# Reordering one pair's attention work beside the projections, and narrower passes for the values' products

## The chip, the cores and the metric

One core of a Trainium2 chip. The metric is the device time of one execution in microseconds (us). TensorE (PE) multiplies and transposes into PSUM; its weight loads are shown as PEld. VectorE (DVE), ScalarE (ACT) and GpSimd (POOL) do elementwise work, SyncE (SP) issues most of the DMAs.

## The reference

A trunk of two layers on one sequence of 512 positions with 1024 features, in float32. Layer 0 mixes by dilated window attention, layer 1 by a short gated convolution; each is followed by a squared-ReLU MLP, and each sub-layer has an RMS norm ahead of it and a residual behind it. The change is in the attention:

```python
qkv = (h @ w_qkv).reshape(B, S, 3, 3, 16, 64)      # group, q/k/v, head, feature
for g in range(3):                                  # dilations 1, 4, 16
    q = partial_rope(rms_norm(qkv[:, :, g, 0], q_gain[g]), cos, sin)
    k = partial_rope(rms_norm(qkv[:, :, g, 1], k_gain[g]), cos, sin)
    num, den, mx = dilated_group(q, k, qkv[:, :, g, 2], dilation[g], radius[g])
w = exp(mx - max over groups of mx)
o = (sum of w * num) / (sum of w * den)
y = o @ w_o
```

`dilated_group` is a softmax over a band of 129 keys (fewer for dilation 16) without its last division: the numerator, the sum of the exponentials and the row maximum.

## The kernel before

Every float32 operand is split into two parts of TensorE's float32r type, `h` (high) and `l` (low), and a product is the sum of three matmuls: high by high, high by low, low by high. ScalarE makes the high part, VectorE the low one (`split`), GpSimd the low one of the weights.

**The stream.** TensorE's main work is a list of units (`add_unit`). A unit is one projection of all 512 rows: eight k-tiles, four row tiles, three matmuls each. Units are cut into blocks of one or two k-tiles, for which weights are loaded (SP's queue) and split ahead. `clock` counts positions: one unit of position is 2048 moving columns by three matmuls, so 16 matmuls of 384 columns (a "projection" below is one of these), or 12 of 512. The 16 heads are taken in 8 pairs; a pair has three units of six positions: A (q of group 0, k of group 0, q of group 1), B (k of group 1, q and k of group 2) and V (the values). Behind pair 7 come the output projections (512 columns), then the MLP, the convolution and the second MLP.

**The tasks.** All other work is put into a heap of tasks with a position (`at`, `put`), and `run_tasks` issues them between the matmuls when their position is reached. Each engine executes in the order of issue, so the positions set the order in every engine's queue. The positions are in `PLACES`: one row for pair 0, one for pairs 1 to 6, one for pair 7. They are counted from the end of A (`tA`) for `sqA`, `rsA`, `mulA`, `TA`, and from the end of B (`tB`, `tS`, the start of V) for the rest. So a pair's attention runs beside its own V and the next pair's A and B.

A pair's tasks, in order: `sqB` squares and row sums; `rsB` (the reciprocal root by Newton steps, 12 small VectorE instructions); `mulB` for four row tiles: the norm product on VectorE (L372), then the rotary step, four small instructions (L377 to L380) on GpSimd for the first `pB` row tiles, on VectorE for the rest, in the buffers `tmpR1` and `tmpR2`, two each; `TB`: transposes and splits of k1, q2, k2 (`qk_fill`, PSUM tiles `st`, three buffers). `S0` twice: scores of group 0 for two of four query blocks, both heads, by matmuls with 64 contraction rows, and on VectorE the masked scores with their maxima (L446); `E0`: exponentials on ScalarE (L465). `X1`, `X2`: maxima and sums of group 0 go from its layout into that of the other groups: `spread` on VectorE (L423), then `swap` on TensorE (L432, 32-column stationary) and a copy; I call this the first exchange. `S12`, `E12`: the same for groups 1 and 2. `W1` to `W4`: the weights of the groups, carried back by a second exchange. `N12`, `N0`: the exponentials times these weights, on GpSimd and VectorE. `PT` (8 times, head `h`, part `i`): four transposes and a split into `pth` and `ptl`; `PV`: the values' products into the single PSUM tile `o`, parts 0 and 1 for group 0 (values `v0`, moved through DRAM), 2 and 3 for groups 1 and 2. The stationary operand of a `PV` matmul is 128 columns wide, high and low half of the values side by side, so that the low half's product comes out in partitions 64 to 127 of `o`; behind a head's last part ScalarE copies those to `tmpO` (L545) and VectorE adds them into `oT` (L546). `qA`, `qB`, `pA`, `pB`, `pN` choose engines, `vA`, `vB` who empties the projections' PSUM (`rawA`, `rawB`).

In pair 0, the setup runs beside it: among it eight fills of the zero halves of k1 and k2 (`zeros`, L269 and L270, VectorE) at positions 9.0 to 11.1. Ahead of the output projections, `split_o` splits `oT`; the last pair's at one position before the end of the first projection unit, directly ahead of the block that reads it.

Of the kernel before, what the change touches and what calls it, by code (L numbers as in the profile page):

```python
# [11 lines left out]
F32 = mybir.dt.float32  # L12
# [23 lines left out]
def _constants():  # L36
# [10 lines left out]
    for n, b in enumerate((0, 1, 3)):  # L47
# [10 lines left out]


PLACES = [  # L60
    dict(sqA=0.52, rsA=0.95, mulA=2.62, dmA=0.05, TA=4.92, dT=0.16, sqB=0.08, rsB=1.22, mulB=1.5, dmB=0.08, TB=4.51, S0=0.4,
         dS=1.15, E0=1.0, X=3.2, lX=0.35, S12=6.05, dS12=0.41, E12=6.8, dE12=0.22, W=8.7, lW=0.25, N12=9.05, N0=9.4, dN=0.04,
         P=10.0, dP=0.75, lP=1.2, qA=0, qB=0, pA=3, pB=3, pN=1, vA=0, vB=8, xq=3.57, dxq=0.29, xs=6.25, lg=2.48, dlg=0.43, tb=4.26, dtb=0.21, gc=8.63),
    dict(sqA=0.02, rsA=0.87, mulA=1.79, dmA=0.28, TA=4.62, dT=0.19, sqB=0.17, rsB=0.8, mulB=1.07, dmB=0.12, TB=3.57,
         S0=0.42, dS=0.92, E0=1.0, X=3.0, lX=0.35, S12=6.0, dS12=0.24, E12=6.6, dE12=0.2, W=8.4, lW=0.25, N12=8.75,
         N0=9.1, dN=0.04, P=9.7, dP=0.75, lP=1.2, qA=0, qB=0, pA=0, pB=3, pN=1, vA=0, vB=12),
    dict(sqA=0.02, rsA=0.8, mulA=1.1, dmA=0.5, TA=4.12, dT=0.02, sqB=0.19, rsB=0.89, mulB=1.15, dmB=0.33, TB=3.4, S0=1.44,
         dS=1.15, E0=2.0, X=4.3, lX=0.3, S12=5.0, dS12=0.25, E12=5.6, dE12=0.2, W=7.3, lW=0.25, N12=7.65, N0=8.0,
         dN=0.04, P=8.4, dP=0.45, lP=0.63, qA=0, qB=0, pA=3, pB=2, pN=1, vA=0, vB=9),
]  # L70


# [1 line left out]
def trunk_kernel(ctx, tc, x, norm1, norm2, wqkv, qgain, kgain, wo, win, conv, wout, w1, w2, c_rope, c_m0, c_m12, out):  # L74
    nc = tc.nc
    pe, act, dve, pool, sync = nc.tensor, nc.scalar, nc.vector, nc.gpsimd, nc.sync
    ctx.enter_context(tc.manual_schedule())

    def ptile(p, shape, dt, name, **kw):
        return p.tile(shape, dt, name=name, **kw)  # L80
# [82 lines left out]
    ab = open_pool("attn", bufs=1)  # L163
# [16 lines left out]
    xs = dram.tile([KT, 128, S], F32, name="xs")  # L180
# [189 lines left out]
    def norm_mul(raw, stt, ng, tab, r, eng):  # L370
        v = raw[r].rearrange("p a (h d) -> p (a h) d", d=64)
        dve.tensor_mul(v, v, stt[:, 2, ng * r:ng * r + ng, None].to_broadcast([128, ng, 64]))  # L372
        rot = v[:, :, 0:16]
        t1 = ptile(ab, [128, 8, 16], F32, "tmpR1", bufs=2)
        t2 = ptile(ab, [128, 8, 16], F32, "tmpR2", bufs=2)
        tb = tab.rearrange("p s r w h d -> p s r (w h) d")
        eng.tensor_mul(t1[:, :ng], rot, tb[:, 0, r])  # L377
        eng.tensor_mul(t2[:, :ng, 0:8], v[:, :, 8:16], tb[:, 1, r, :, 0:8])  # L378
        eng.tensor_mul(t2[:, :ng, 8:16], v[:, :, 0:8], tb[:, 1, r, :, 8:16])  # L379
        eng.tensor_add(rot, t1[:, :ng], t2[:, :ng])  # L380
# [36 lines left out]

    N0, D0, N0S, N12, D0S, D12, F0S, F12, NM, EX, F0 = 0, 1, 2, 3, 4, 5, 6, 7, 8, 9, 12

# [14 lines left out]

    def S0(bp):
        ps = [ptile(psT, [128, 512], F32, "st") for _ in range(2)]
# [6 lines left out]
        for h in range(2):  # L443
            for b2 in range(2):
                b = 2 * bp + b2
                dve.tensor_tensor_reduce(out=sm0[:, h, b], in0=ps[h][:, 256 * b2:256 * b2 + 256],  # L446
                                         in1=msk0[:, (0, 1, 1, 2)[b]], scale=1.0, scalar=3.0e38, op0=ALU.add, op1=ALU.min,
                                         accum_out=mx(N0)[:, 4 * h + b:4 * h + b + 1])

# [43 lines left out]
    def weights_back(p):  # L493
        ps = swap(st[p].pop("sp1"), 8)
        dve.tensor_copy(mx(F0).rearrange("p (h b) -> p h b", h=2), ps)
# [28 lines left out]
    def PV(p, h, i, first, last):  # L524

        hi, lo = st[p].pop(("pt", h, i))
        if first:
            st[p]["o"] = ptile(psO, [128, 512], F32, "o")
        o = st[p]["o"]
        ops = []  # L530
        if i < 2:
            for j in (2 * i, 2 * i + 1):
                ov = o.rearrange("p (r b c) -> p b r c", r=4, c=32)
                ov = ov[:, j:j + 2] if j < 3 else ov[:, 0:4:3]
                ops += [(ov, st[p]["v0"][:, j, h], t[:, 256 * (j % 2):256 * (j % 2) + 256]) for t in (hi, lo)]
        else:
            v = st[p]["v"].rearrange("p r g h s d -> p r g h (s d)")
            for r in range(4):
                c = slice(128 * r, 128 * r + 128)
                ops += [(o[:, c], v[:, r, i - 1, h], t[:, c]) for t in (hi, lo)]  # L540
        for q, (out_, stat, mov) in enumerate(ops):
            pe.matmul(out_, stat, mov, start=first and q == 0, stop=last and q == len(ops) - 1, skip_group_check=True)  # L542
        if last:
            t1 = ptile(ab, [64, 512], F32, "tmpO")
            act.copy(t1, o[64:128])  # L545
            dve.tensor_add(oT[p][64 * h:64 * h + 64], o[0:64], t1)  # L546
# [38 lines left out]
    def attn_tasks(p, tA, tB, c):  # L585


        tS = tB

        def put(pos, name, fn, *needs):  # L590
            def go():
                for n in needs:
                    need(*n)
                fn()
                mark(name, p)
            at(pos, go)

        for r in range(4):
            put(tA + c["sqA"] + 0.25 * r, "sqA", lambda r=r: norm_sq(rawA, stA, 6, r, r < c["qA"]), ("evA", p, 4))
        put(tA + c["sqA"] + c["rsA"], "rsA", lambda: norm_rs(stA, 6), ("sqA", p, 4), ("stats", 0, 1))  # L600
        for r in range(4):
            put(tA + c["mulA"] + c["dmA"] * r, "mulA", lambda r=r: norm_mul(rawA, stA, 6, tabA, r, pool if r < c["pA"] else dve), ("rsA", p, 1), ("tables", 0, 6))
        for i, nm in enumerate(("q0", "k0", "q1")):
            put(tA + c["TA"] + c["dT"] * i, "TA", lambda i=i, nm=nm: qk_fill(rawA, i, nm, i), ("mulA", p, 4), ("cols", 0, 1),
                ("S0", p - 1, 2), ("S12", p - 1, 4))
        for r in range(4):
            put(tB + c["sqB"] + 0.25 * r, "sqB", lambda r=r: norm_sq(rawB, stB, 6, r, r < c["qB"]), ("evB", p, 4))
        put(tB + c["sqB"] + c["rsB"], "rsB", lambda: norm_rs(stB, 6), ("sqB", p, 4))
        for r in range(4):
            put(tB + c["mulB"] + c["dmB"] * r, "mulB", lambda r=r: norm_mul(rawB, stB, 6, tabB, r, pool if r < c["pB"] else dve), ("rsB", p, 1))  # L610
        for i, nm in enumerate(("k1", "q2", "k2")):
            put(tB + c["TB"] + c["dT"] * i, "TB", lambda i=i, nm=nm: qk_fill(rawB, i, nm, 3 + i), ("mulB", p, 4),
                ("S12", p - 1, 4))
        for i in range(2):
            put(tS + c["S0"] + c["dS"] * i, "S0", lambda i=i: S0(i), ("TA", p, 3), ("PT", p - 1, 8), ("gains", 0, 11))
            for n in range(4):
                put(tS + c["E0"] + c["dS"] * i + 0.15 * n, "E0", lambda i=i, n=n: exps(0, n // 2, 2 * i + n % 2), ("S0", p, i + 1))

        def sp0():
            st[p]["sp0"] = spread(mx(N0, 2), 16)  # L620

        put(tS + c["X"], "X1", sp0, ("E0", p, 8), ("perm", 0, 1))
        put(tS + c["X"] + c["lX"], "X2", lambda: stats_over(p), ("X1", p, 1), ("N0", p - 1, 8))
        for r in range(4):
            put(tS + c["S12"] + c["dS12"] * r, "S12", lambda r=r: S12(r), ("TB", p, 3), ("PT", p - 1, 8))
            for h in range(2):
                put(tS + c["E12"] + c["dE12"] * (2 * r + h), "E12", lambda h=h, r=r: exps(1, h, r), ("S12", p, r + 1))
        w = tS + c["W"]
        put(w, "W1", weigh1, ("E12", p, 8), ("X2", p, 1))
        put(w + 0.1, "W2", weigh2, ("W1", p, 1))  # L630
        put(w + c["lW"], "W3", lambda: weigh3(p), ("W2", p, 1))
        put(w + c["lW"] + c["lX"], "W4", lambda: weights_back(p), ("W3", p, 1))
        for n in range(8):
            put(tS + c["N12"] + c["dN"] * n, "N12", lambda n=n: pnorm(1, n // 4, n % 4, n % 4 >= c["pN"]), ("W3", p, 1))
            put(tS + c["N0"] + c["dN"] * n, "N0", lambda n=n: pnorm(0, n // 4, n % 4, n % 4 >= c["pN"]), ("W4", p, 1))
        for n, (h, i) in enumerate(((0, 2), (0, 3), (0, 0), (0, 1), (1, 2), (1, 3), (1, 0), (1, 1))):
            s = tS + c["P"] + c["dP"] * n
            put(s, "PT", lambda h=h, i=i: PT(p, h, i), ("N12" if i > 1 else "N0", p, 8))
            put(s + c["lP"], "PV", lambda h=h, i=i, n=n: PV(p, h, i, n % 4 == 0, n % 4 == 3), ("PT", p, n + 1), ("evV", p, 4),
                ("v0", p, 1))  # L640
# [3 lines left out]
    c = PLACES[0]  # L644
# [317 lines left out]
    for i, b in enumerate(blocks):  # L962
# [4 lines left out]
        ops = b["emit"]([ready.pop(b["first"] + q) for q in range(b["n"])])  # L967
# [28 lines left out]
```

## Time and profile before

| | us |
|---|---|
| median of 3 timed runs | 1557.04 (1555.07 to 1557.34) |
| the profiled execution, its time | 1546.28 |
| its span, first to last instruction | 1544.2 |
| TensorE busy | 1486.8 |
| VectorE busy | 679.4 |
| ScalarE busy | 662.8 |
| GpSimd busy | 725.5 |

Times within the trace count from the span's start. Matmuls are pipelined: a row's duration is longer than the distance from its start to the next start, and the distance is what it costs. An idle time in brackets names what ended it. L numbers are lines of the kernel.

### The profile page before, as it was taken

Reading aid. Unit: us, or ns where it says so; the run is one execution under the profiler, and the core shown is the slowest. Engines: PE = TensorE matmul, PEld = TensorE weight load, DVE = VectorE, ACT = ScalarE, POOL = GpSimd, SP = SyncE. Lnnn points to the kernel's source line nnn. Section 1 sums busy time; section 2 is a strip of 40 time slices with the busy share of each in tenths; the row PEclk is TensorE's granted clock in tenths of the full one; section 3 lists DMA queues with packets and bytes.
Section 4 is the critical chain, followed back from the end, with each engine's and each line's share of the span. In section 5 each row is a group of like instructions: output and inputs, shape, how many; then the busy total and the mean of one; then the engine's idle time right before and its main releaser. Section 6 shows DMA issues by size and latency. Waiting matters only on the chain.

```text
span 1544.2 us, 22344 instructions
## 1 busy us (share of the span) xinstructions
PE 1486.8 (96%) x7772; PEld 1302.1 (84%) x7772; DVE 679.4 (44%) x1522; ACT 662.8 (43%) x1364; POOL 725.5 (47%) x760
## 2 busy tenths in 40 slices
PE   8799999999999988999999999999999999999998
PEld 8699999999999987788888888888887888888887
DVE  5747565656657475363112131474347420121222
ACT  5355564645555545444433242343334443433320
POOL 3544444445363554354445444445544444444542
PEclk9899999999999999999999999999999999999999
DMA  5432323222232322433332333233332233233332
GB/s 141 140 90 62 100 66 91 83 85 87 75 93 59 100 78 75 134 97 96 94 98 96 96 96 99 89 86 93 105 116 84 89 103 96 96 96 96 96 96 82
DMA packets 163292, 144.75 MB, mean 94 GB/s; under 512 B 13748, under 2 KB 123116, under 8 KB 163180
## 3 DMA queue, kind: packets, MB, share of 16 engines
q1 hardware_dynamic: 162892, 143.06, 30.7%
q8 instruction: 61, 1.00, 0.3%
q14 instruction: 51, 0.42, 0.1%
q10 hardware_dynamic: 288, 0.27, 0.1%
HBM read 134.89 MB, written 8.39 MB: 93 GB/s over the span
## 4 chain that ended last, share of the span: by engine, by line
PE 77%; issue 8%; DVE 7%; POOL 4%; DMA 1%; ACT 1%; SPq 1%; POOLq 0%; ACTq 0%; DVEq 0%
PE g L127 71%; POOL wl L292 2%; PE o L542 2%; PE st L456 1%; PE st L515 1%; PE st L389 1%; DMA wraw<-in_a_wqkv 1%; POOL tmpR L377 1%; DVE sqa L698 0%; DVE spread L423 0%; SPq L565 0%; POOL tmpR L379 0%; POOL tmpR L378 0%; DVE hgBl L700 0%; DMA sm<-in_x 0%
## 5 line engine op out<-in xcount | busy, mean ns | idle before, releaser
L292 POOL TENSOR_TENSOR wl<-wraw,wh 128x512 fp32r<-128x512 f32 (+1 forms) x542 | 636.8, 1196 | 737.0 <-ACT wh L291 729.3
L291 ACT CAST wh<-wraw 128x512 fp32r<-128x512 f32 (+1 forms) x542 | 297.6, 570 | 493.6 <-PE g L127 398.4
L127 PE MATMUL g<-hgBh,wl 128*128 128x512 f32 x704 | 274.6, 390 | 0.0
L127 PE MATMUL g<-hgBh,wh 128*128 128x512 f32 x704 | 274.6, 390 | 0.0
L127 PE MATMUL g<-hgBl,wh 128*128 128x512 f32 x704 | 274.4, 390 | 0.0
L127 PE MATMUL g<-wh,hgh 128*128 128x384 f32 x768 | 267.0, 348 | 0.1
L127 PE MATMUL g<-wl,hgh 128*128 128x384 f32 x768 | 265.8, 346 | 0.0
L127 PE MATMUL g<-wh,hgl 128*128 128x384 f32 x768 | 262.8, 342 | 1.9 <-DVE hgl L306 1.7
L788 DVE SCALAR_TENSOR_TENSOR zr<-g,R 128x512 f32<-128x512 f32 x64 | 44.1, 691 | 293.1 <-PE g L127 293.0
L127 PEld LDWEIGHTS g<-hgBh,wl 128*128 128x128 f32 x704 | 132.5, 188 | 27.8
L127 PEld LDWEIGHTS g<-hgBh,wh 128*128 128x128 f32 x704 | 132.5, 188 | 27.6
L127 PEld LDWEIGHTS g<-hgBl,wh 128*128 128x128 f32 x704 | 132.6, 188 | 27.5
L127 PEld LDWEIGHTS g<-wh,hgl 128*128 128x128 f32 x768 | 146.1, 190 | 3.2 <-DVE hgl L306 3.0
L127 PEld LDWEIGHTS g<-wl,hgh 128*128 128x128 f32 x768 | 146.2, 190 | 2.0
L127 PEld LDWEIGHTS g<-wh,hgh 128*128 128x128 f32 x768 | 145.8, 190 | 1.2 <-ACT hgh L304 0.4
L805 DVE TENSOR_TENSOR acc<-g,acc 128x512 f32<-128x512 f32 x32 | 22.1, 691 | 138.2 <-PE g L127 138.2
L292 DVE TENSOR_TENSOR ptl<-st,pth 128x512 fp32r<-128x512 f32 x64 | 44.1, 689 | 79.2 <-ACT pth L291 78.7
L291 ACT CAST pth<-st 128x512 fp32r<-128x512 f32 x64 | 37.6, 587 | 95.4 <-PE st L515 95.3
L465 ACT ACTIVATE sm<-sm,mxs 128x256 f32<-128x256 f32 x128 | 63.7, 499 | 27.5 <-DVE mxs L446 24.0
L127 PE MATMUL g<-z0h,wh 128*128 128x512 f32 x192 | 74.7, 389 | 0.0
L127 PE MATMUL g<-z0l,wh 128*128 128x512 f32 x192 | 74.7, 389 | 0.0
L127 PE MATMUL g<-z0h,wl 128*128 128x512 f32 x192 | 74.7, 389 | 0.0
(222 smaller groups left out, 2369.9 us busy)
## 6 DMA issues: line engine op xcount, KB each, us to landing
wraw<-in_mlp_w SPq DMA_DIRECT2D x256, 256.0 KB
wraw<-in_a_wqkv SPq DMA_DIRECT2D x128, 128.0 KB
wraw<-in_a_wqkv SPq DMA_DIRECT2D x64, 192.0 KB
wraw<-in_a_wqkv SPq DMA_DIRECT2D x128, 64.0 KB
wraw<-in_b_win SPq DMA_DIRECT2D x64, 128.0 KB
v0d<-v SPq DMA_DIRECT2D x8, 512.0 KB
v<-v0d SPq DMA_DIRECT2D x64, 64.0 KB
wraw<-in_a_wo SPq DMA_DIRECT2D x16, 256.0 KB
```

What stands on the lines that cost most here:

```text
L127: pe.matmul(unit["ps"][n][:, :width], a, b, start=st, stop=sp)
L291: act.copy(hi, src)
L292: (eng or dve).tensor_sub(lo, src, f32(hi))
L377: eng.tensor_mul(t1[:, :ng], rot, tb[:, 0, r])
L389: pe.transpose(o, raw[r][:, w, :], ident)
L456: pe.matmul(pv[:, :, g], a[:, 128 * r:128 * r + 128], k[:, 256 * r:256 * r + 256], start=(q == 0), stop=(q == 2))
L465: act.activation(t[:, h, b], t[:, h, b], AF.Exp, bias=mx(m)[:, c], scale=-1.0, accum_out=mx(d)[:, c])
L515: pe.transpose(ps[:, 128 * n:128 * n + 128], src, ident)
L542: pe.matmul(out_, stat, mov, start=first and q == 0, stop=last and q == len(ops) - 1, skip_group_check=True)
L788: dve.scalar_tensor_tensor(zr, ps, 0.0, state["R"], op0=ALU.max, op1=ALU.mult)
L805: dve.tensor_add(a, ps, a)
```

## The change

`PLACES` gets new positions: the second `S0` comes 0.50 to 0.55 positions behind the first (before 0.92 to 1.15) and so ahead of `mulB`; the exchange, `TA`, `TB`, `S12`, `W`, `N12`, `N0`, `PT` and `PV` come later; a new `lF` is the distance from W3 to W4, a new `gP` an extra distance ahead of head 1's parts. The rotary step on GpSimd gets its own `tmpR` buffers. The parts of a head come in the order 0, 1, 2, 3 (before 2, 3, 0, 1). In parts 2 and 3 each of the four column blocks of `o` gets three matmuls with a 64-column stationary operand into partitions 0 to 63 (high by high, high by low, low by high) in place of two with 128 columns; the product of the two low parts, which the 128-column form adds, falls away there.

```diff
 PLACES = [
-    dict(sqA=0.52, rsA=0.95, mulA=2.62, dmA=0.05, TA=4.92, dT=0.16, sqB=0.08, rsB=1.22, mulB=1.5, dmB=0.08, TB=4.51, S0=0.4,
-         dS=1.15, E0=1.0, X=3.2, lX=0.35, S12=6.05, dS12=0.41, E12=6.8, dE12=0.22, W=8.7, lW=0.25, N12=9.05, N0=9.4, dN=0.04,
-         P=10.0, dP=0.75, lP=1.2, qA=0, qB=0, pA=3, pB=3, pN=1, vA=0, vB=8, xq=3.57, dxq=0.29, xs=6.25, lg=2.48, dlg=0.43, tb=4.26, dtb=0.21, gc=8.63),
-    dict(sqA=0.02, rsA=0.87, mulA=1.79, dmA=0.28, TA=4.62, dT=0.19, sqB=0.17, rsB=0.8, mulB=1.07, dmB=0.12, TB=3.57,
-         S0=0.42, dS=0.92, E0=1.0, X=3.0, lX=0.35, S12=6.0, dS12=0.24, E12=6.6, dE12=0.2, W=8.4, lW=0.25, N12=8.75,
-         N0=9.1, dN=0.04, P=9.7, dP=0.75, lP=1.2, qA=0, qB=0, pA=0, pB=3, pN=1, vA=0, vB=12),
-    dict(sqA=0.02, rsA=0.8, mulA=1.1, dmA=0.5, TA=4.12, dT=0.02, sqB=0.19, rsB=0.89, mulB=1.15, dmB=0.33, TB=3.4, S0=1.44,
-         dS=1.15, E0=2.0, X=4.3, lX=0.3, S12=5.0, dS12=0.25, E12=5.6, dE12=0.2, W=7.3, lW=0.25, N12=7.65, N0=8.0,
-         dN=0.04, P=8.4, dP=0.45, lP=0.63, qA=0, qB=0, pA=3, pB=2, pN=1, vA=0, vB=9),
+    dict(sqA=0.52, rsA=0.95, mulA=2.62, dmA=0.05, TA=6.3, dT=0.2, sqB=0.08, rsB=1.22, mulB=1.8, dmB=0.1, TB=5.0, S0=1.05,
+         dS=0.5, E0=2.1, X=4.2, lX=0.6, S12=7.2, dS12=0.3, E12=7.9, dE12=0.2, W=9.5, lW=0.35, lF=0.9, N0=10.85, N12=9.95,
+         dN=0.04, P=11.4, dP=0.62, gP=0.4, lP=1.7, qA=0, qB=0, pA=3, pB=3, pN=1, vA=0, vB=8, xq=3.57, dxq=0.29, xs=6.25,
+         lg=2.48, dlg=0.43, tb=4.26, dtb=0.21, gc=8.63),
+    dict(sqA=0.02, rsA=0.87, mulA=1.79, dmA=0.28, TA=4.8, dT=0.19, sqB=0.17, rsB=0.8, mulB=1.07, dmB=0.12, TB=3.9,
+         S0=0.45, dS=0.55, E0=1.1, X=3.1, lX=0.5, S12=6.5, dS12=0.24, E12=7.1, dE12=0.2, W=8.9, lW=0.35, lF=0.9, N0=10.25,
+         N12=9.4, dN=0.04, P=10.9, dP=0.66, gP=0.4, lP=1.7, qA=0, qB=0, pA=0, pB=3, pN=1, vA=0, vB=12),
+    dict(sqA=0.02, rsA=0.8, mulA=1.1, dmA=0.5, TA=4.5, dT=0.1, sqB=0.19, rsB=0.89, mulB=1.15, dmB=0.2, TB=3.9, S0=0.45,
+         dS=0.55, E0=1.1, X=3.1, lX=0.5, S12=6.0, dS12=0.24, E12=6.5, dE12=0.18, W=8.0, lW=0.3, lF=0.7, N0=9.1, N12=8.4,
+         dN=0.03, P=9.5, dP=0.36, gP=0.2, lP=0.7, qA=0, qB=0, pA=3, pB=2, pN=1, vA=0, vB=9),
 ]
...
-        t1 = ptile(ab, [128, 8, 16], F32, "tmpR1", bufs=2)
-        t2 = ptile(ab, [128, 8, 16], F32, "tmpR2", bufs=2)
+        of = "P" if eng is pool else ""
+        t1 = ptile(ab, [128, 8, 16], F32, "tmpR1" + of, bufs=2)
+        t2 = ptile(ab, [128, 8, 16], F32, "tmpR2" + of, bufs=2)
...
-                ops += [(o[:, c], v[:, r, i - 1, h], t[:, c]) for t in (hi, lo)]
+                vh, vl = v[:, r, i - 1, h, 0:64], v[:, r, i - 1, h, 64:128]
+                ops += [(o[0:64, c], a, t[:, c]) for a, t in ((vh, hi), (vh, lo), (vl, hi))]
...
-        put(w + c["lW"] + c["lX"], "W4", lambda: weights_back(p), ("W3", p, 1))
+        put(w + c["lW"] + c["lF"], "W4", lambda: weights_back(p), ("W3", p, 1))
...
-        for n, (h, i) in enumerate(((0, 2), (0, 3), (0, 0), (0, 1), (1, 2), (1, 3), (1, 0), (1, 1))):
-            s = tS + c["P"] + c["dP"] * n
+        for n, (h, i) in enumerate([(h, i) for h in range(2) for i in range(4)]):
+            s = tS + c["P"] + c["dP"] * n + c["gP"] * (n > 3)
```

## Rows read from the trace of the kernel before

**Rows 1.** The page, busy time (share of the span) and instructions.
```profile
PE 1486.8 (96%) x7772; PEld 1302.1 (84%) x7772; DVE 679.4 (44%) x1522; ACT 662.8 (43%) x1364; POOL 725.5 (47%) x760
```
**Rows 2.** TensorE's waits, whole span: total us, times, longest.
```profile
PE st L432 <- DVE spread L423: 23.9, 9, 5.1
...
PE st L389 <- POOL rawA L380: 4.6, 3, 2.3
```
**Rows 3.** TensorE's waits from 90 to 560 us, all there are.
```profile
PE st L432 <- DVE spread L423: 13.3, 6, 2.2
PE o L542 <- DVE oT L546: 9.3, 6, 1.6
```
**Rows 4.** TensorE in order of time around a first exchange: start us, us.
```profile
359.22 0.34 PE L127 MATMUL g<-wh,hgl 128*128 128x384 f32 x1
361.77 0.26 PE L432 MATMUL st<-spread,fold 128*32 128x16 f32 x8 [2.21 <-DVE spread L423]
361.95 0.44 PE L127 MATMUL g<-wh,hgh 128*128 128x384 f32 x1
362.24 0.34 PE L127 MATMUL g<-wl,hgh 128*128 128x384 f32 x1
```
**Rows 5.** VectorE in order of time ahead of that exchange.
```profile
355.17 1.70 DVE L372 TENSOR_TENSOR rawB<-rawB,stB 128x384 f32<-128x384 f32 x3
356.79 0.41 DVE L446 CUSTOM_DVE_ANT_0 sm<-st,msk 128x256 f32<-128x256 f32 x1
...
358.16 0.58 DVE L372 TENSOR_TENSOR rawB<-rawB,stB 128x384 f32<-128x384 f32 x1
359.39 0.43 DVE L377 TENSOR_TENSOR tmpR<-rawB,tabB 128x96 f32<-128x96 f32 x1 [0.65 <-POOL rawB L380]
...
360.70 1.01 DVE L423 TENSOR_TENSOR spread<-mxs,quad 128x64 f32<-128x64 f32 x1
```
**Rows 6.** VectorE in order of time, the add of head 0.
```profile
330.71 0.67 DVE L546 TENSOR_TENSOR oT<-o,tmpO 64x512 f32<-64x512 f32 x1
```
**Rows 7.** TensorE in order of time, head 1's first product and what follows it.
```profile
331.44 0.33 PE L542 MATMUL o<-pth,v 128*128 128x128 f32 x1 [1.58 <-DVE oT L546]
...
332.39 0.39 PE L127 MATMUL g<-wl,hgh 128*128 128x384 f32 x1
```
**Rows 8.** The chain that ended last, a stretch of projections alone: start us, us.
```profile
150.19 5.55 PE g L127 x32
```
**Rows 9.** Windows of the first and last pair: length, busy, granted clock, DMA.
```profile
66.00:80.00 14.00, 8.92 (x52) 8.49 (x51) 7.05 (x24) 4.41 (x13) 7.22 (x16) 0.76 0.21 57
560.00:640.00 80.00, 69.15 (x388) 59.88 (x387) 47.31 (x112) 40.95 (x93) 33.22 (x40) 0.94 0.31 101
```
**Rows 10.** VectorE in order of time, the sixth of the eight fills.
```profile
55.02 0.48 DVE L270 MEMSET k2h<- 64x512 f32 x1
```
**Rows 11.** TensorE's waits from 560 to 640 us.
```profile
PE st L432 <- DVE spread L423: 5.5, 2, 4.3
PE st L389 <- DVE rawB L380: 3.1, 1, 3.1
```
**Rows 12.** TensorE in order of time around a first S0.
```profile
348.86 0.34 PE L127 MATMUL g<-wh,hgh 128*128 128x384 f32 x1
349.13 0.39 PE L442 MATMUL st<-k0h,q0h 64*128 64x256 f32 x2
349.35 0.28 PE L442 MATMUL st<-k0l,q0h 64*128 64x256 f32 x2
...
349.82 0.28 PE L442 MATMUL st<-k0h,q0l 64*128 64x256 f32 x2
...
350.32 0.34 PE L127 MATMUL g<-wh,hgl 128*128 128x384 f32 x1
```
**Rows 13.** Groups by line and form, weight loads: busy us, mean ns, idle before.
```profile
L542 PEld LDWEIGHTS o<-ptl,v 128*128 128x128 f32 x192 | 36.5, 190 | 0.3
...
L432 PEld LDWEIGHTS st<-spread,fold 128*32 128x32 f32 x128 | 2.6, 109 | 28.6 <-DVE spread L423 25.3 <-issue 3.3
```

## The prediction

> **What bounds the kernel now.** I read the page first: TensorE is busy 96% of the span [rows 1], so only time in which it stands still, or the length of its own instructions, can matter. Then its waits: the exchange of group 0's maxima (`swap`, L432) waits 23.9 us for VectorE's `spread`, the transposes (L389) 4.6 us for GpSimd's rotary steps [rows 2]. Cut to 90 to 560 us, six periods of one pair each (71.7 us from exchange to exchange), two waits are left, each six times: the exchange's 13.3 us, and 9.3 us of the values' products (L542) for the copy of the output bank, `oT` [rows 3]. As lost time, against the spacing without a wait, they are 2.38 us and 1.74 us a pair, 24.7 us in six pairs. The rest lies at the two ends: the first pair (before 90 us) and the last (560 to 640 us). From 640 us on (MLPs, convolution) the change issues nothing.
>
> Why the exchange waits: TensorE comes to it at 359.4, its `spread` runs from 360.70 to 361.71 [rows 4, 5]. VectorE did nothing slow for it; it did other things first: three norm products (1.70 us) ahead of the second half of group 0's maxima (356.79), the fourth norm product, 0.65 us of waiting for GpSimd's rotary step, since both share the two `tmpR` buffers, and its own rotary step until 360.7 [rows 5].
>
> Why the products wait: the bank `o` is single. The first product of head 1 follows the last of head 0 by 0.75 position units (12 projections of 0.174 us, and a transpose), and VectorE's add to `oT` stands behind the norm's row sums and Newton steps until 330.71 [rows 6]; the product starts at 331.44, after 1.58 us of idle [rows 7].
>
> Positions: a unit is 16 projections of 384 columns; 32 of them take 5.55 us [rows 8], so 0.174 us each and 2.78 us a unit without other work. Each term below is a change against the profiled execution (span 1544.2, time 1546.28 us); that execution is 10.8 us below the median of the timed runs, and I carry the sum over to the median 1557.04.
>
> **The exchange, pairs 1 to 6.** The second half of the scores moves from position 1.34 to 1.0, so on VectorE its four maxima (1.37 us) come ahead of the norm products, behind the Newton steps that end at 355.17. New order: maxima to 356.6, four products of 0.56 to 358.9, its rotary step at once (own buffers; 0.9 to 1.4 us, the latter beside GpSimd [rows 5]) to 360.1, `spread` 0.3 to 1.0 us: ready at 360.6 to 361.1. ScalarE's four exponentials behind the maxima end near 358.6, so they don't hold it. TensorE comes later, at 3.6 instead of 3.35: 4 projections, 0.69 us, at 360.1, first matmul 360.2. Loss 0.4 to 0.9 us instead of 2.38; the later product at 17.62 also delays VectorE's copy of `rawB` by 0.2 us. I take 1.6 us won, **-9.6 us** in six pairs (bounds 0, should `spread` slip as far as TensorE, and -14.3). Next late: GpSimd's rotary steps start 1.4 us later and end near 361.9; the transposes that need them move from 3.57 to 3.9, which TensorE reaches near 362. That fits, barely. GpSimd's weight splits behind them slip as much, and are needed at 4.5, past 365.
>
> **The output bank, pairs 1 to 6.** `gP` and `dP` make 0.75 units 1.06: 17 projections (2.95 us) and two transposes of four matmuls, 0.44 us each at 0.111 [rows 7], 3.8 us. The add now stands behind `ptl` splits and three norm steps (a product of 0.56 and a rotary step of 0.9 to 1.4, as in rows 5), all emitted before position 14.58; placing these in order from the end of the A projections I get the add done about 1.4 us ahead of its reader at 15.64. So all of it goes: **-10.4 us** (bounds 0 and -10.4). The order of the products changes too: group 0's come first, so they read weights that need the second exchange (W4, 10.15) and the norm steps N0; TensorE reaches the exchange 3 us behind its `spread`, and the first transpose at 10.9 about 0.6 us behind the two GpSimd steps of half a microsecond it needs. No wait, with little to spare.
>
> **The first pair.** Before: 4.6 us on `rawA` and 5.1 us on `spread` [rows 2], 1.2 us at k2, and the clock: 66 to 80 us has a mean granted clock of 0.76 [rows 9], so it stood at its lower level (1.2 GHz) for nearly half, behind the wait; about 2 us lost after 74. After: the transposes at 6.3 come 3.8 us later, and wait 1.5 us. But q0 and k0 now stand behind all eight fills of the zero halves, the sixth of which ends at 55.5 [rows 10]; k0 is ready at 59.4, where TensorE has waited since 54.5. It is then 1.4 us later than now and 1.8 us of projections further. `spread` ends near 72.6, 1.5 us sooner, with TensorE 3.5 us further. 5.0 won at the exchange, 2.0 of clock and 1.2 at k2, less 1.7 for a lower clock behind the new 4.9 us wait: **-6.5 us** (-2 to -11).
>
> **The last pair.** Before: 3.1 us at `rawB` and 0.6 behind it, 5.5 us at the two exchanges [rows 11] (5.9 as lost time), 2.4 at the last split, and a mean clock of 0.94 over 560 to 640 [rows 9], some 10 us at the lower level in three stretches, 1.7 us lost in each: 17 us. After: the exchange 3.2 (both rotary steps on VectorE beside GpSimd), the second 0.7 (3.0 units behind the first S12, which now runs after the splits of `oT`), the first transpose 1.0 (N12 and N0 both on GpSimd before it), the last split 4.7: its product moves from 12.18 to 12.92, directly ahead of its reader at 13.0, where now 0.8 units of projections lie between. With two stretches of lower clock, 13.0: **-4 us** (+3 to -10).
>
> **The values' products.** For groups 1 and 2, 8 matmuls with 128 stationary columns become 12 with 64, both of 128 moving columns; 32 such products in all. Before: 331.44 to 332.39 for eight [rows 7], 0.111 us each behind the first, 0.89 us. No row has a 64-column stationary of 128 rows. Bound below: spacing falls by 0.056 us from 384 moving columns (0.174 [rows 8]) to 256 (0.118, four steps from 349.35 to 349.82 [rows 12]), so to about 0.065 us for 128 if the load hides; the loads' rows (128 columns 190 ns, 32 columns 109 ns [rows 13]) put 64 columns at 135, 55 ns shorter, so it hides. Bound above: 0.111. I take 0.065, since the load is what fell. But the other stationary shapes pay for the change of shape: S0 (64 rows) takes from 348.86 to 350.32 what two projections (0.35) and six steps of 0.118 (0.71) explain to 1.06, so 0.40 us go at entry and exit [rows 12]; behind the 32-column exchange too the second projection comes 0.29 us after the first, not 0.174 [rows 4]. The old product, of the projections' own shape, pays nothing. I take 0.34 (a shorter first load): 12 x 0.065 + 0.34 = 1.12 us, +0.23 each, **+7.4 us** (no shape cost: -3.5; 0.111 a pass and 0.34: +25). The transposes, copies, DMAs and SP's queue issue the same as before.
>
> The Trainium skill (TensorE: Matmul & The Clock Gate, LDWEIGHTS) says that a load takes time by its columns, not its rows, about 107 ns for 128 and 53 for 64. The spacing of 0.111 us agrees with the first; by it without the shape cost the sum would be that of rival B.
>
> **Sum:** -9.6 -10.4 -6.5 -4 +7.4 = -23.1 us: 1557.04 becomes **1534 us**; the profiled execution 1523.
>
> **Rivals.**
> A. As above, 1534, chance 0.53 (own range 1527 to 1542).
> B. The narrow passes pay no change of shape: -3.5 instead of +7.4, 1523. For it: the columns alone set the load. Against it: both other shapes pay. 0.15.
> C. A narrow pass takes as long as a wide one, 0.111 us, plus the shape: +25, 1552. For it: 0.111 could be a floor for any pair of load and matmul. Against it: the eight matmuls of the exchange take 0.18 us to the next projection [rows 4]. 0.11.
> D. The exchange's wait only moves: `spread` slips with the rotary steps, or the transposes wait for GpSimd; then the first and fourth terms are nothing: 1548. 0.12.
> E. Slower: in the narrow shape no load runs beside a matmul, so each pass pays what the first step of S0 pays, 0.22 us [rows 12], less 0.05 for half the columns, 0.17: 12 x 0.17 + 0.2 = 2.24, +1.35 each, +43, net +12.5, 1570. It decides from 0.13 us a pass, where +1.0 x 32 eats the other 30.5. For it: that first step. Against it: the later S0 steps, 0.118 us for 256 columns, leave no room for a load. 0.09.
> The skill's rule that a load overlaps running matmuls only in other row groups (same page, The mechanism) would give E; projections 0.174 us apart on the same rows, with loads of 0.19, speak against it.
>
> **Range and chances.** 0.2% of 1557 is 3.1 us, about what runs of this kernel can tell. Low end: B with the exchange's wait wholly gone, 1518; high end: C, 1552. E and the worst of D and C lie outside. Faster: A, B and most of C and D, 0.82; same: the upper edge of C and D, 0.08; slower: E and a little more, 0.10.
>
> **What the trace would show.** L432's waits under 1 us in pairs 1 to 6; no wait of L542 for `oT`; on VectorE maxima ahead of norm products, no wait for GpSimd's rotary; a new wait of some 5 us at the first S0, and of 4.7 us ahead of the last output-projection block; twelve narrow passes in 1.1 us. Passes over 0.1 us, or waits of the first PT on N0 or of L389 on GpSimd in every pair, would make me wrong.

## The result and the profile after

| | before | after |
|---|---|---|
| median of the timed runs, us | 1556.05 (1545.17 to 1557.34, 4 runs) | 1536.7 (1533.39 to 1538.26, 4 runs) |
| ratio | | 0.9888 (95%: 0.984 to 0.9936) |
| the profiled execution, us | 1546.28 | 1538.26 |
| its span, us | 1544.2 | 1536.4 |

Faster, 19 us by the medians, against the forecast of 1534. A second set of runs gave 1534.83 against 1550.67, 0.9904 (0.9882 to 0.9927). The two profiled spans differ by only 7.8 us, and that difference is what the traces can explain. The rest comes from the kernel before, whose time varies with the clock that TensorE is granted (below).

Busy time of the changed kernel, the page's first part:

```profile
PE 1488.8 (97%) x7900; PEld 1296.0 (84%) x7900; DVE 693.0 (45%) x1522; ACT 664.4 (43%) x1364; POOL 727.6 (47%) x760
```

TensorE has 128 instructions more than in [rows 1] (32 products, four passes more each) and is busy 2 us longer. Its waits from 90 to 560 us, to be held against [rows 3]:

```profile
PE o L545 <- DVE oT L549: 6.9, 6, 1.6
PE g L128 <- DVE v L296: 4.8, 6, 0.8
PE st L517 <- POOL sm L503: 4.3, 7, 2.9
PE st L391 <- POOL rawB L382: 2.3, 6, 0.4
PE st L434 <- DVE spread L425: 0.2, 1, 0.2
```

The exchange's 13.3 us have become 0.2. But `oT` kept 6.9 of its 9.3, and three waits are new: the projections wait for VectorE's copy of the values, the transposes of the weights (PT) for GpSimd's norm steps N0, and the transposes of `rawB` for GpSimd's rotary steps. Where the exchange stood at [rows 4], TensorE now reads, in order of time:

```profile
358.96 0.34 PE L128 MATMUL g<-wh,hgh 128*128 128x384 f32 x1
359.31 0.26 PE L434 MATMUL st<-spread,fold 128*32 128x16 f32 x8
359.50 0.45 PE L128 MATMUL g<-wl,hgh 128*128 128x384 f32 x1
```

and VectorE ahead of it, against [rows 5]:

```profile
354.27 0.42 DVE L448 CUSTOM_DVE_ANT_0 sm<-st,msk 128x256 f32<-128x256 f32 x1
...
355.65 2.25 DVE L373 TENSOR_TENSOR rawB<-rawB,stB 128x384 f32<-128x384 f32 x4
357.93 0.26 DVE L379 TENSOR_TENSOR tmpR<-rawB,tabB 128x96 f32<-128x96 f32 x1
...
358.95 0.31 DVE L425 TENSOR_TENSOR spread<-mxs,quad 128x64 f32<-128x64 f32 x1
```

The maxima come first, then four norm products, the rotary step without a wait, and a `spread` of 0.31 us instead of 1.01.

A values' product of head 0 in 64-column passes (compare [rows 7]):

```profile
327.16 0.22 PE L545 MATMUL o<-pth,v 128*64 128x128 f32 x1
327.22 0.22 PE L545 MATMUL o<-ptl,v 128*64 128x128 f32 x1
...
327.81 0.22 PE L545 MATMUL o<-pth,v 128*64 128x128 f32 x1
327.88 0.39 PE L128 MATMUL g<-wl,hgh 128*128 128x384 f32 x1
```

Twelve passes run from 327.16 to 327.88: 0.72 us, 0.060 each. Nothing is paid for the change of shape: the last projection ahead starts at 326.98, one projection's 0.18 us before the first pass, and the projection behind is followed by the next after 0.23 us, as it is behind a product of 128 columns in the kernel before.

The add to `oT`, VectorE in order of time:

```profile
332.56 0.55 DVE L373 TENSOR_TENSOR rawA<-rawA,stA 128x384 f32<-128x384 f32 x1
333.14 0.95 DVE L379 TENSOR_TENSOR tmpR<-rawA,tabA 128x96 f32<-128x96 f32 x1
334.01 1.02 DVE L380 TENSOR_TENSOR tmpR<-rawA,tabA 128x48 f32<-128x48 f32 x1
...
335.36 0.68 DVE L549 TENSOR_TENSOR oT<-o,tmpO 64x512 f32<-64x512 f32 x1
```

GpSimd in the same stretch, and TensorE's reader of the bank:

```profile
332.89 2.08 POOL L293 TENSOR_TENSOR wl<-wraw,wh 128x384 fp32r<-128x384 f32 x2 [5.12 <-ACT wh L292]
```
```profile
334.70 0.34 PE L128 MATMUL g<-wl,hgh 128*128 128x384 f32 x1
336.10 0.39 PE L545 MATMUL o<-pth,v 128*128 128x256 f32 x1 [1.06 <-DVE oT L549]
```

The first two instructions of this rotary step take 0.95 and 1.02 us, where the same forms take 0.26 and 0.20 in the two steps before it. Each ends about 0.1 us after one of GpSimd's two splits (1.09 and 1.03 us, the first from 332.89). The Trainium skill (SBUF — State Buffer, "SBUF: two separate sides") says that VectorE, with two operands from SBUF, and a GpSimd instruction that reads SBUF hold a port pair in turn, each for a whole instruction; these rows agree.

**Pair by pair.** By the start of the same projections, before to after. The forecast's +7.4 for the 32 values' products is shared out by their number, 4, 24 and 4:

| stretch | forecast, us | measured, us |
|---|---|---|
| first pair, up to the values of pair 1 | -5.6 | +1.7 |
| pairs 1 to 6, up to the values of pair 7 | -14.4 | -6.5 |
| last pair, and what follows | -3.1 | -3.0 |
| sum | -23.1 | -7.8 |

The second profile of the changed kernel (after_again) has +1.4, -6.3 and -4.3.

A middle period of 71.70 us became 70.78. As lost time at TensorE, from distances between starts less the spacing without a wait: exchange 2.38 to 0.18, -2.20; `oT` 1.74 to 1.22, -0.52; narrow passes -0.5 (together_wide below); `rawB` +0.60; the values' copy +0.97; PT on N0 +0.71; together -0.94, where the period shows -0.92.

By the traces, the wait on the values' copy comes from two moves that meet; neither was run alone. In the kernel before, the score products of groups 1 and 2 (`S12`, position 6.0) stand at the end of the values' unit and fill 0.71 us; at position 6.5 they no longer do. Before, at the end of a values' unit, and after:

```profile
298.99 0.28 PE L456 MATMUL st<-k1h,q1h 128*128 128x256 f32 x1
...
299.70 0.34 PE L127 MATMUL g<-wh,hgh 128*128 128x384 f32 x1
```
```profile
369.11 0.44 PE L128 MATMUL g<-wh,hgh 128*128 128x384 f32 x1 [0.80 <-DVE v L296]
```

And the copies stand in ScalarE's queue behind the splits of `TB`, which start 0.33 positions later, so they begin 0.9 us later against the unit's last projection.

In the first pair, waits from 40 to 130 us, and windows (length, busy by engine, granted clock, DMA) of two stretches:

```profile
PE g L128 <- POOL wl L293: 3.6, 2, 3.5
PE st L517 <- POOL sm L503: 2.9, 1, 2.9
PE o L545 <- DVE oT L549: 1.6, 1, 1.6
PE st L444 <- ACT k0h L295: 1.6, 1, 1.6
PE g L128 <- DVE v L296: 1.6, 1, 1.6
```
```profile
66.00:80.00 14.00, 14.00 (x92) 13.57 (x90) 9.94 (x29) 7.90 (x19) 8.55 (x16) 1.00 0.25 71
90.00:110.00 20.00, 17.05 (x92) 16.18 (x91) 5.90 (x17) 8.79 (x22) 11.46 (x18) 0.83 0.33 96
```

The old wait on `rawA` and that of the exchange are gone, and 66 to 80 us runs at full clock (0.76 in [rows 9]). In their place the projections wait for a weight split behind GpSimd's rotary steps, and PT for N0 behind two other splits. Behind that wait the granted clock falls: a mean of 0.83 over 20 us is 6.8 us at its lower level (1.2 GHz), 3.4 us lost. GpSimd in order of time:

```profile
99.15 1.95 POOL L293 TENSOR_TENSOR wl<-wraw,wh 128x384 fp32r<-128x384 f32 x2 [2.11 <-ACT wh L292]
101.07 1.84 POOL L503 TENSOR_SCALAR sm<-sm,mxs 128x256 f32<-128x256 f32 x4
```

**Median and span.** Runs of the kernel before that were timed beside the experiments took 1556.0 to 1556.8 us where the mean granted clock was 0.983, and 1544.2 to 1545.5 at 0.991 and 0.992. The changed kernel's ten runs have 0.991 to 0.995 and 1533.4 to 1538.3. At one clock the change is thus worth some 8 us, as the spans say; the rest of the median's gain is that the changed kernel is granted the lower level less often. Which edit does that, and where in the kernel before the lower level falls in its long runs, is not shown: none of those has a trace.

### The profile page after: what moved, and what is told of

It is laid out like the page before. It is cut to its first block, busy times and chain, and to the rows that moved or that the text cites. A ratio compares the mean times of both kernels' runs of the same rounds, so it can differ in the third digit from the quotient of the medians.

```text
span 1536.4 us, 22581 instructions
## 1 busy us (share of the span) xinstructions
PE 1488.8 (97%) x7900; PEld 1296.0 (84%) x7900; DVE 693.0 (45%) x1522; ACT 664.4 (43%) x1364; POOL 727.6 (47%) x760
## 3 DMA queue, kind: packets, MB, share of 16 engines
q8 instruction: 62, 1.02, 0.3%
## 4 chain that ended last, share of the span: by engine, by line
PE 59%; DVE 2%; issue 0%; DMA 0%; ACT 0%; POOL 0%; DVEq 0%
PE g L128 58%; DVE sqa L701 1%; DVE hgBl L703 0%; PE o L545 0%; PE st L517 0%; DVE hT L922 0%; PE g L855 0%; DMA out<-zr 0%; DVE zr L921 0%; PE g L715 0%; POOL sm L503 0%; DVE zr L814 0%; ACT sgh L292 0%; PE g L714 0%; DVE hgl L293 0%
```

## The experiments

Each expectation states its own theories. The question behind the first four runs: which of the edits took the exchange's wait, and what did the others cost? "After" is the changed kernel, and periods are taken from projection to projection in the middle pairs.

**wide_products.** The products back in 128 columns.
```diff
-                vh, vl = v[:, r, i - 1, h, 0:64], v[:, r, i - 1, h, 64:128]
-                ops += [(o[0:64, c], a, t[:, c]) for a, t in ((vh, hi), (vh, lo), (vl, hi))]
+                ops += [(o[:, c], v[:, r, i - 1, h], t[:, c]) for t in (hi, lo)]
```


> The changed kernel with the values' products of groups 1 and 2 back to two matmuls of 128 stationary columns for each column block (8 instead of 12 a product), all else as changed. Theory 1 (from the changed kernel's trace: a narrow pass takes 0.060 us and pays nothing at its ends, so a product takes 0.72 us instead of 0.89): undoing it costs 0.17 us for each of 32 products, +5.5 us in all, and a middle pair's period goes from 70.78 to about 71.45 us. Theory 2 (the prediction's step: narrow passes pay 0.34 us for the change of shape): undoing it wins 7.4 us, the period falls to about 69.9.

1537.99 us (1536.83 to 1542.52), ratio 0.9924 (0.9898 to 0.9949) to the kernel before; span 1537.5, period 71.20, +0.42 a pair. The narrow passes win; the forecast's sign was wrong. The size is disturbed by the waits of this kernel, so it was measured again below (together_wide).

**late_maxima.** The second half of the scores in pairs 1 to 6 at the old distance.
```diff
 PLACES[1]
-dS=0.55
+dS=0.92
```


> The changed kernel with one number back, for pairs 1 to 6: dS=0.92, so the second half of group 0's scores and its maxima stand behind three of the norm products again. Theory 1: the order of maxima and norm products does not move the spread, since VectorE has the same work ahead of it either way and the exponentials end in time; what it moves is GpSimd's start on the rotary steps, 1.4 us earlier here. So the exchange's wait stays near 0.2 us, the new wait of the k1 transposes on GpSimd (0.6 us a pair) goes, the one of the next unit's first matmul on the copy of the values (1.0) shrinks or goes: period 69.2 to 70.1 instead of 70.78, 4 to 9 us faster than the changed kernel. Theory 2 (the prediction's): the order is what took the exchange's wait away; it comes back with 1 us or more a pair, period 71.8 or more, 6 us slower.

1532.67 us (1530.96 to 1533.26), 0.9888 (0.986 to 0.9915); span 1530.9, 5.5 us shorter than after. TensorE's waits from 90 to 560 us:

```profile
PE o L545 <- DVE oT L549: 6.9, 6, 1.6
PE g L128 <- DVE v L296: 4.8, 6, 0.8
PE st L517 <- POOL sm L503: 4.4, 7, 3.1
PE st L434 <- DVE spread L425: 0.2, 1, 0.2
```

With the maxima behind the norm products again the exchange still doesn't wait, and the row of `rawB` is gone. Moving the maxima ahead buys nothing and delays the products that GpSimd's rotary steps need: 0.54 us a pair, 3.3 us in the middle pairs. The other parts of the 5.5 us are no work of the edit: what follows the values of pair 7 is 3.4 us shorter, with a granted clock of 1.00 from 605 to 650 us where after has 0.92, and the first pair is 1.1 us longer.

**shared_rotary.** All of the change but the own buffers.
```diff
-        of = "P" if eng is pool else ""
+        of = ""
```


> The changed kernel with one pair of rotary buffers shared by GpSimd and VectorE again. Theory 1: VectorE's rotary step of the fourth row tile waits for the end of GpSimd's second one, which the new order has made 1.4 us later than before: about 2 us of waiting, nearly all of it seen by the exchange behind the spread; period 72.3 to 72.8. Theory 2 (the prediction's): only the 0.65 us that this wait took before; period near 71.4, or no change if the exchange has that much to spare.

1560.28 us (1558.29 to 1564.14), 1.0076 (1.005 to 1.0102): slower than before. VectorE in order of time:

```profile
298.53 0.42 DVE L379 TENSOR_TENSOR tmpR<-rawB,tabB 128x96 f32<-128x96 f32 x1 [1.95 <-POOL rawB L382]
...
299.85 1.01 DVE L425 TENSOR_TENSOR spread<-mxs,quad 128x64 f32<-128x64 f32 x1
```

The rotary step waits 1.95 us for GpSimd's, and `spread` then meets GpSimd's splits and takes 1.01. TensorE waits 3.0 us at an exchange on average (3.1 at most), and from 225 to 375 us the mean granted clock is 0.95. The period is 3 to 4.3 us longer than after's, more than the wait by itself.

**norms_behind_add.** All four of VectorE's norm steps behind the add to `oT`.
```diff
 PLACES[1]
-mulA=1.79
+mulA=2.59
```


> The changed kernel with one number moved, for pairs 1 to 6: mulA=2.59 instead of 1.79, so the next pair's norm and rotary steps stand behind the add of head 0 into oT on VectorE instead of three of the four ahead of it. Theory 1: the wait of head 1's first product on oT (1.22 us in five pairs, 1.81 in the first) is VectorE's queue order alone; it goes, period 69.6, 7 to 8 us faster than the changed kernel. Rival: the norm steps end too late and the transposes of rawA wait instead, by about as much; period unchanged.

1534.78 us (1531.11 to 1535.38), 0.9898 (0.9869 to 0.9928); span 1529.3. The row of `oT` is gone and this one is there instead, five times:

```profile
PE st L391 <- DVE rawA L382: 7.4, 5, 1.5
```

So the rival is right: the wait moved to the transposes of `rawA`, and in pairs 2 to 6 the period is 0.4 us longer. The span is 7.1 us shorter all the same, by the two ends: 6.1 us in the first pair, where the wait for `oT` (1.8) is gone and the granted clock is 1.00 from 90 to 110 us (0.83 in after), and 3.4 us behind the values of pair 7, with 1.00 from 605 to 650 us (0.92 in after). So two steps instead of four:

**two_behind_add.**
```diff
 PLACES[1]
-dmA=0.28
+dmA=0.5
```


> Two of the four norm steps of VectorE (r2, r3) go behind its add to oT, not none (after: span 1536.4) and not all four (1529.3, where the rawA transposes came to wait 1.64 us a pair). Theory 1: the wait of the values' products for oT (1.22 us in each of pairs 2 to 6, 1.81 in the first) goes because the add has two slow rotary steps fewer ahead of it, and rawA is still in time because only two steps are late: period about 69.6 us, not 70.78, span about 1528 to 1529.5. Rival: half-way is no cure; the oT wait halves and a rawA wait of about half a microsecond comes in, period 70.4 to 70.8, span 1534 to 1536.

1524.24 us (1523.83 to 1525.69), 0.9835 (0.9807 to 0.9864); span 1522.0. Waits from 90 to 560 us, all of them:

```profile
PE g L128 <- DVE v L296: 4.8, 6, 0.8
PE st L517 <- POOL sm L503: 4.6, 7, 3.2
PE st L391 <- POOL rawB L382: 2.3, 6, 0.4
PE st L434 <- DVE spread L425: 0.2, 1, 0.2
```

Neither `oT` nor `rawA`: the period is 69.5, as theory 1 has it. The span is 6 us shorter than that theory gave. 2.4 us of the gain come behind the last pair's exchange, where the theory had nothing and the granted clock is higher (0.96 from 605 to 650 us, 0.92 in after). The first pair wins 5.3 us, not 1.8: the stretch from 90 to 110 us, with its PT wait no shorter, has a granted clock of 1.00 where after had 0.83. Two executions of the changed kernel itself differ there too (0.83, and 0.91 in after_again), so this part can't be put down to the edit; the period can.

**first_pair_weights.** N0 ahead of the weight split on GpSimd, in the first pair.
```diff
 PLACES[0]
-lF=0.9, N0=10.85
+lF=0.3, N0=10.2
```


> In the first pair alone the eight norm steps N0 are issued ahead of the last weight split, so that on GpSimd no split that waits for ScalarE's cast stands ahead of them. Theory 1: the 3.1 us that the first transpose of the weights (PT) waits for GpSimd at 98.4 goes, and with it the stretch of lower clock of 6.8 us behind it (3.4 us lost): span up to 6.5 us shorter than after (1530 or more). Rival: the lower clock comes from the idle time of the whole first pair, not from this wait, and the wait is taken up by the next reader (oT, 1.8 us): span within 2 us of after's 1536.4.

1532.3 us (1530.68 to 1533.5), 0.9885 (0.9858 to 0.9911); span 1528.8, 7.6 us below after's, of which 4.1 are won in the first pair and the rest behind the last pair's exchange, which the edit doesn't touch (granted clock 1.00 from 605 to 650 us, 0.92 in after). Windows from 90 to 130 us, and the `oT` row of 90 to 560 us:

```profile
90.00:110.00 20.00, 20.00 (x139) 19.34 (x138) 11.02 (x30) 10.49 (x26) 13.52 (x20) 1.00 0.41 117
110.00:130.00 20.00, 17.05 (x124) 16.35 (x123) 12.74 (x31) 7.05 (x14) 4.08 (x4) 0.91 0.16 47
```
```profile
PE o L545 <- DVE oT L549: 8.2, 6, 2.9
```

The wait on N0 and the lower clock behind it are gone, but TensorE comes earlier to `oT`, waits 2.9 us there instead of 1.6, and the clock falls behind that wait instead: a mean of 0.91 from 110 to 130 us, where after has 1.00. Both theories hold in part: some of the wait, and about half of the time at the lower level, moved on to the next reader.

**own_buffers_alone.** The kernel before, with one edit.
```diff
-        t1 = ptile(ab, [128, 8, 16], F32, "tmpR1", bufs=2)
-        t2 = ptile(ab, [128, 8, 16], F32, "tmpR2", bufs=2)
+        of = "P" if eng is pool else ""
+        t1 = ptile(ab, [128, 8, 16], F32, "tmpR1" + of, bufs=2)
+        t2 = ptile(ab, [128, 8, 16], F32, "tmpR2" + of, bufs=2)
```


> The kernel before with one edit, the rotary steps' own buffers for GpSimd. Theory 1 (the shared buffers were the larger part of the exchange's wait): VectorE's rotary step no longer waits 0.65 us for GpSimd's and its steps run without its hand-overs, so the exchange (2.38 us lost a pair) loses 1.3 to 1.7; period 71.70 becomes 70.6 to 71.05, span 1538 to 1540, and the median falls further than the span, to 1540 to 1545, where fewer stretches of lower clock follow the shorter wait. Rival (the order of the maxima and the later reader are what took the wait): at most the 0.65 us of waiting is won, period 71.05 or more, span 1540 or more, median about 1550.

1539.95 us (1533.99 to 1541.65), 0.9929 (0.9902 to 0.9955); span 1532.7, below after's. The median is not: six of its eight runs have a granted clock of 0.983 to 0.985 and take 1538.6 to 1541.7 us, and the profiled one has 0.990. Waits from 90 to 560 us, VectorE ahead of an exchange, and TensorE there:

```profile
PE o L543 <- DVE oT L547: 9.3, 6, 1.6
PE st L433 <- DVE spread L424: 3.5, 6, 0.6
```
```profile
208.85 0.26 DVE L378 TENSOR_TENSOR tmpR<-rawB,tabB 128x96 f32<-128x96 f32 x1
...
209.87 0.30 DVE L424 TENSOR_TENSOR spread<-mxs,quad 128x64 f32<-128x64 f32 x1
```
```profile
210.22 0.26 PE L433 MATMUL st<-spread,fold 128*32 128x16 f32 x8 [0.60 <-DVE spread L424]
```

In the old order, with three norm products still ahead of the maxima, 1.64 of the exchange's 2.38 us are gone, and the period is 70.06 where the clock is full. By [rows 5]: 0.65 us of waiting, 0.29 of a quicker rotary step (1.31 to 1.02), and 0.71 of a `spread` that takes 0.30 because it now ends before GpSimd's splits begin; 1.65 in all. Two later periods took 71.65 us, at a mean granted clock of 0.98 and with the same waits, so the lower clock came there without a longer wait. In the first pair, too, this one edit takes 3.5 us off the exchange's wait (5.1 to 1.6), and the values of pair 1 start 4.9 us sooner than before; in after they start 1.7 us later.

**own_and_narrow.** The same, and the narrow passes in the old order (the first pass of a bank stays wide).
```diff
+                vh, vl = v[:, r, i - 1, h, 0:64], v[:, r, i - 1, h, 64:128]
+                if first and r == 0:
+                    ops += [(o[:, c], v[:, r, i - 1, h], hi[:, c]), (o[0:64, c], vh, lo[:, c])]
+                else:
+                    ops += [(o[0:64, c], a, t[:, c]) for a, t in ((vh, hi), (vh, lo), (vl, hi))]
```


> The kernel before with two edits: the rotary steps' own buffers for GpSimd, and the values' products in 64-column passes (the very first pass of a bank stays 128 columns wide, since it opens the bank). All positions stay those of before. Theory 1 (the positions of the change cost more than they bring): period between the 70.06 of own_buffers_alone and 69.4 (four products of 0.17 a pair saved, those ahead of the oT wait swallowed by it), so below after's 70.78, and span 1527 to 1533, below after's 1536.4. Rival (the positions are needed for the narrow passes, or a narrow pass pays a change of shape beside wide ones): period 70.5 or more, span 1536 or more.

1526.41 us (1525.06 to 1528.51), 0.9847 (0.9822 to 0.9873); span 1525.1, period 69.46. Two edits of the change, without any of its positions and with the parts of a head in the old order, are 8.4 us faster than the whole change timed in the same set (after_again, 1534.83). Its two waits that return in each pair, from 90 to 560 us:

```profile
PE o L547 <- DVE oT L551: 9.3, 6, 1.6
PE st L433 <- DVE spread L424: 3.5, 6, 0.6
```

The old waits of `oT` and a short one at the exchange remain; the new positions take 1.1 us a pair off these two (1.74 to 1.22 and 0.75 to 0.18) and add 2.3 in the three new ones.

**together.** After, with late_maxima, two_behind_add, first_pair_weights, `rawB`'s transposes at 3.65 and N0 evenly on two engines.
```diff
 PLACES[0]
-lF=0.9, N0=10.85
+lF=0.3, N0=10.2
 PLACES[1]
-dmA=0.28, TB=3.9, dS=0.55
+dmA=0.5, TB=3.65, dS=0.92
...
-pnorm(0, n // 4, n % 4, n % 4 >= c["pN"])
+pnorm(0, n // 4, n % 4, n % 4 >= 2)
```


> The changed kernel with what the runs so far speak for: the second half of group 0's scores back at 1.37 (0.54 us a pair won in late_maxima), two norm steps behind the add, rawB's transposes at 3.65 in place of 3.9, two of every four norm steps N0 on GpSimd instead of three, and the first pair's N0 ahead of its last weight split. Theory 1 (the waits are separate): the ledger adds up, -3.3 for the maxima, -4 to -8 for oT, -4 for PT on GpSimd (0.71 a pair), -3 to -6 in the first pair: span 1512 to 1520. Rival (each wait taken away hands its time to the next reader): half of it or less, span 1525 or more.

1515.64 us (1512.85 to 1516.39), 0.9775 (0.9746 to 0.9804); span 1513.4, period 67.84. Waits from 90 to 560 us, all of them:

```profile
PE st L434 <- DVE spread L425: 2.4, 2, 2.2
PE o L545 <- DVE oT L549: 1.5, 1, 1.5
```

The 2.2 us stand at an exchange of the last pair (550.97), the 1.5 us in the first pair. In the middle pairs the exchange, the values' copy and PT have 0.1 us of idle time or less each, too short for the view. There the waits were separate: of the 3.0 us that the period lost, late_maxima alone gave 0.54 and two_behind_add alone 1.3, and the rest belongs to the two edits that were not run alone. In the first pair the gains do not add: two_behind_add alone won 5.3 us, first_pair_weights alone 4.1, and together wins 5.1. This kernel is the fastest of all that were timed.

**together_wide.** Together, with the products in 128 columns, as in wide_products.

> Kernel together with the values' products back in two passes of 128 columns, nothing else. In together nothing waits in the middle pairs, so no wait can swallow the difference. Theory 1 (a pass of 64 columns takes 0.060 us and pays nothing for the change of shape, a pass of 128 takes 0.111): 0.17 us for each of the 32 products, period 67.83 becomes 68.5, span 1513.4 becomes about 1519. Rival (the prediction's price of 0.34 us for the change of shape, which the trace of after might hide in waits): period 66.9, span about 1506.

1519.37 us (1516.06 to 1519.98), 0.9795 (0.9769 to 0.982); span 1517.3, period 68.34: +0.50 a pair, four products, 0.12 us each. That is 48 passes at 0.060 us (2.89 by the starts) against 32 at 0.105 (3.36). Theory 1 in sign, three quarters of its size, since a wide pass took 0.105 on average and not 0.111.

**after_again.** After, unaltered.

> The changed kernel once more, unaltered, beside the other two: what its time is on the same chip and in the same call. Theory 1: 1536.7 us within 0.2%, period 70.78, exchange, oT, rawB, PT and v waits as in the first trace; its stretches of lower clock near 53 and 101 us and at the end may come and go, which moves its span by up to 5 us. Rival (the first trace was an odd execution): another period or other waits in the middle pairs.

1534.83 us (1533.92 to 1537.02), 0.9904 (0.9882 to 0.9927); span 1534.9, period 70.83, the same waits in the middle pairs.

## Why the prediction was right, and where it was not

The time, the sign and case A's range came true (1536.7 against 1534, own range 1527 to 1542). The sum did not: it put the profiled execution at 1523, and that was 1538.26. That the time came true was luck. A sum 15 us too good was made up by the step that carries it to the median: the 10.8 us between the profiled execution and the median of before were kept as if they belonged to both kernels. By the granted clocks of the runs they were time at the lower level, which the changed kernel is granted less often. Term by term:

- **The exchange, -9.6.** The wait went as forecast, and the term was undersized: 2.20 us a pair, not 1.6 (-13.2 in six). The working took the edits as one and gave the order of the maxima a part in it; that order buys nothing (late_maxima). Of the 2.20 the own buffers alone bring 1.64, with no help from another edit, and without them the rest makes the kernel slower than before (shared_rotary). The 0.56 that are left fit the later reader, which by the forecast comes 0.69 us later; no run shows it by itself. I allowed `spread` 0.3 to 1.0 us; that it would miss GpSimd's splits, 0.71 us, was the largest single part of the buffers' gain.
- **"That fits, barely".** It did not: the transposes of `rawB` wait 0.60 us a pair, because the maxima moved ahead delay the norm products (late_maxima takes it away). This was named as what would make the forecast wrong.
- **The output bank, -10.4.** The step that failed most: 0.52 us of 1.74 went, -3.1. The add was placed 1.4 us ahead of its reader, and it ended 1.2 us behind the time at which TensorE could have gone on (1.06 idle). A norm step met two GpSimd splits, and two of its short instructions took 1.97 us; with two norm steps fewer ahead of the add the wait is gone (two_behind_add). The two instructions explain 1.5 us of the 2.6 between forecast and trace; the rest of the misplacing stays open.
- **"No wait, with little to spare"** at PT on N0: 0.71 us a pair. The wait on the values' copy, 0.97, was not foreseen at all. By the traces it takes both the later `S12` and the later `TB`; it stays in late_maxima and two_behind_add, and falls to 0.27 in together, where `TB` comes 0.25 positions (0.7 us) sooner and `S12` is unchanged. Neither move was run alone.
- **The first pair, -6.5.** Measured +1.7. The exchange's wait and the lower clock behind it went as forecast, and the new wait at S0 came, 1.6 us instead of 4.9. But 3.5 us at a GpSimd split, 2.9 at N0 with the lower clock behind it, 1.6 at `oT` and 1.6 at the values' copy came as well. The view of before showed none of these queues as late, and I asked of each moved step only what it waits for, not what GpSimd then has ahead of what.
- **The last pair, -4.** -3.0, with other parts: the exchanges 2.26 and 2.30 as lost time, the values' copy 1.17, PT 1.31, the last split 2.97, and a granted clock of 0.92 from 605 to 650 us.
- **The values' products, +7.4.** Wrong in sign. The pass was right (0.060, forecast 0.065); the price of 0.34 for the change of shape is not there. Rival B had this mechanism, with -3.5. Measured: 0.12 us saved a product in together_wide, 0.15 between own_buffers_alone and own_and_narrow (0.60 a pair), so -4 to -5 us for 32. The price came from S0 with its 64 rows, and half the columns behave otherwise.
- **Rival D** held in part: three new waits in every pair gave back 2.3 us, about the size of the exchange's gain. **Rivals C and E** fell with the pass of 0.060.

## What to carry to other kernels

When a change moves several steps and separates a shared buffer, price the buffer alone first: here one buffer edit and the narrow passes are worth 24 us by the medians (19 by the spans), and the new positions and order of parts took 8 of them back. A step that is moved ahead on one engine must be followed to every queue behind it, GpSimd's among them, because there a reader met a split that was itself waiting. And a gain found on one profiled execution isn't simply carried to the median of runs: the runs of one kernel differ in the clock they are granted, and with it in time, here by 13 us in the kernel before and by 5 in the changed one; so compare executions at one clock.

## What the runs showed of the chip that was not expected

- Short VectorE operations on two SBUF operands ended about 0.1 us behind the GpSimd split beside which they started, however short they are otherwise: 0.95, 1.02 and 1.01 us instead of 0.20 to 0.31. Whether `spread` starts before or after GpSimd's splits is worth 0.7 us.
- A pass with 64 stationary columns and 128 moving columns costs 0.060 us here, one with 128 stationary columns 0.105, and the change between the two shapes costs nothing. S0, with 64 rows, does pay [rows 12]; a shape isn't priced by another shape.
- Where the lower clock falls differs between two executions of one kernel with the same waits in the middle pairs: after and after_again have 1.00 and 0.94 from 60 to 90 us, 0.83 and 0.91 from 90 to 110, 1.00 and 0.91 from 565 to 605. Worked out from these clocks, each such difference is 1.6 to 3.6 us lost or not. So two_behind_add, with a PT wait in its first pair of 3.2 us against 2.9 in after and a granted clock of 1.00 behind it, doesn't show what keeps the clock up.
